# Local attention in windows of 64: tokens moved in groups of 512, stores moved to the loads' queue

## The chip, the cores and the metric

One Trainium2 chip, one of its cores. The metric is device time in microseconds (us), lower is better. Engines: PE (matmul), DVE (VectorE), ACT (ScalarE), POOL (GpSimd), SP (SyncE), and 16 DMA engines. The runs were made in several calls, on different chips: the median of the kernel before moved between 973.7 and 974.3 us, so differences under 1 us between calls are not read.

## The reference

```python
B, S, D, W = 4, 4096, 1536, 64           # q, k, v: float32 [B, S, D]
logits = einsum('bnwd,bnud->bnwu', q_w, k_w) * D ** -0.5   # inside each window of 64 tokens
attn = softmax(logits)
out = einsum('bnwu,bnud->bnwd', attn, v_w)                 # float32 [B, S, D]
```

There is little arithmetic per byte: 302 MB are read and 101 MB written, 402.7 MB together.

## The kernel before

A step handles a pair of windows, 128 tokens. GpSimd issues the three loads, which cast float32 to bf16 on the way. PE transposes q and k in chunks, DVE and ACT evict the transposes from PSUM, PE makes logits, ACT the exponentials, PE the product with v, DVE and ACT scale it, and SP issues the store.

```python
qkv_pool = tile_pool(name="qkv", bufs=3)
for b in range(B):
    for p in range(n_pairs):
        s0 = p * PAIR
        ...
        nc.gpsimd.dma_start(out=q_nat, in_=q[b, s0 : s0 + PAIR, :])   # [128, D] bf16 <- f32
        nc.gpsimd.dma_start(out=k_nat, in_=k[b, s0 : s0 + PAIR, :])
        nc.gpsimd.dma_start(out=v_nat, in_=v[b, s0 : s0 + PAIR, :])
        ...                                     # 24 transposes into tp, eight to a PSUM tile
            if g % 2 == 0: nc.vector.tensor_copy(qk_t[:, lo:hi, :], tp[:, : hi - lo, :])
            else:          nc.scalar.copy(qk_t[:, lo:hi, :], tp[:, : hi - lo, :])
        ...                                     # logits, exp, sum, product with v, scaling
        nc.sync.dma_start(out=out[b, s0 : s0 + PAIR, :], in_=o_sb)
```

The softmax here doesn't subtract the row's maximum and nothing guards it: scores larger than these inputs give would overflow.

Of the kernel before, what the change touches and what calls it, by code (L numbers as in the profile page):

```python
# [1 line left out]

# [5 lines left out]


FP32 = mybir.dt.float32
BF16 = mybir.dt.bfloat16


@with_exitstack
def kernel(
    ctx: ExitStack,
    tc: tile.TileContext,
    q: bass.AP,
    k: bass.AP,  # L20
    v: bass.AP,
    out: bass.AP,
):
    nc = tc.nc

    B, S, D = q.shape
    W = 64
    PAIR = 2 * W
    n_pairs = S // PAIR
    n_chunks = D // 128  # L30
    n_out_chunks = D // 512
    scale = float(D) ** -0.5

    consts = ctx.enter_context(tc.tile_pool(name="consts", bufs=1))
    qkv_pool = ctx.enter_context(tc.tile_pool(name="qkv", bufs=3))
    qkt_pool = ctx.enter_context(tc.tile_pool(name="qkt", bufs=2))
    attn_pool = ctx.enter_context(tc.tile_pool(name="attn", bufs=4))
    out_pool = ctx.enter_context(tc.tile_pool(name="outp", bufs=3))

    tp_psum = ctx.enter_context(tc.tile_pool(name="tp_psum", bufs=3, space=bass.MemoryType.PSUM))  # L40
    s_psum = ctx.enter_context(tc.tile_pool(name="s_psum", bufs=2, space=bass.MemoryType.PSUM))
    u_psum = ctx.enter_context(tc.tile_pool(name="u_psum", bufs=3, space=bass.MemoryType.PSUM))

    ident = consts.tile([128, 128], BF16)
    make_identity(nc, ident)

    maskt = consts.tile([128, 128], BF16)
    nc.gpsimd.memset(maskt, -100000.0)
    nc.gpsimd.memset(maskt[0:64, 0:64], 0.0)
    nc.gpsimd.memset(maskt[64:128, 64:128], 0.0)  # L50

    ones = consts.tile([128, 1], BF16)
    nc.gpsimd.memset(ones, 1.0)

    for b in range(B):
        for p in range(n_pairs):
            s0 = p * PAIR

            q_nat = qkv_pool.tile([128, D], BF16, name="q_nat")
            k_nat = qkv_pool.tile([128, D], BF16, name="k_nat")  # L60
            v_nat = qkv_pool.tile([128, D], BF16, name="v_nat")
            nc.gpsimd.dma_start(out=q_nat, in_=q[b, s0 : s0 + PAIR, :])  # L62
            nc.gpsimd.dma_start(out=k_nat, in_=k[b, s0 : s0 + PAIR, :])  # L63
            nc.gpsimd.dma_start(out=v_nat, in_=v[b, s0 : s0 + PAIR, :])  # L64

            qk_t = qkt_pool.tile([128, 2 * n_chunks, 128], BF16, name="qk_t")
            n_groups = (2 * n_chunks + 7) // 8
            for g in range(n_groups):
                lo = g * 8
                hi = min(lo + 8, 2 * n_chunks)  # L70
                tp = tp_psum.tile([128, 8, 128], BF16, name="tp")
                for c in range(lo, hi):
                    if c < n_chunks:
                        src = q_nat[:, c * 128 : (c + 1) * 128]
                    else:
                        cc = c - n_chunks
                        src = k_nat[:, cc * 128 : (cc + 1) * 128]
                    nc.tensor.transpose(tp[:, c - lo, :], src, ident)  # L78
                if g % 2 == 0:
                    nc.vector.tensor_copy(qk_t[:, lo:hi, :], tp[:, : hi - lo, :])  # L80
                else:
                    nc.scalar.copy(qk_t[:, lo:hi, :], tp[:, : hi - lo, :])  # L82

            s_ps = s_psum.tile([128, 132], FP32, name="s_ps")
            st = s_ps[:, 0:128]
            for j in range(n_chunks):
                nc.tensor.matmul(  # L87
                    st,
                    qk_t[:, n_chunks + j, :],
                    qk_t[:, j, :],  # L90
                    start=(j == 0),
                    stop=False,
                )
            nc.tensor.matmul(st, ident, maskt, start=False, stop=True)  # L94

            p_t = attn_pool.tile([128, 128], BF16, name="p_t")
            nc.scalar.activation(  # L97
                out=p_t,
                in_=st,
                func=mybir.ActivationFunctionType.Exp,  # L100
                scale=scale,
            )

            nc.tensor.matmul(s_ps[:, 128:129], p_t, ones, start=True, stop=True)  # L104
            r_recip = attn_pool.tile([128, 1], FP32, name="r_recip")
            nc.vector.reciprocal(r_recip, s_ps[:, 128:129])  # L106

            o_sb = out_pool.tile([128, D], FP32, name="o_sb")
            for c in range(n_out_chunks):
                u_ps = u_psum.tile([128, 512], FP32, name="u_ps")  # L110
                nc.tensor.matmul(  # L111
                    u_ps,
                    p_t,
                    v_nat[:, c * 512 : (c + 1) * 512],
                    start=True,
                    stop=True,
                )
                o_slice = o_sb[:, c * 512 : (c + 1) * 512]
                if c % 2 == 0:
                    nc.scalar.mul(o_slice, u_ps, r_recip)  # L120
                else:
                    nc.vector.tensor_scalar_mul(o_slice, u_ps, r_recip)  # L122

            nc.sync.dma_start(out=out[b, s0 : s0 + PAIR, :], in_=o_sb)


# [1 line left out]
_INS = ['q', 'k', 'v']  # L128
_OUTS = [((4, 4096, 1536), 'float32')]


# [23 lines left out]
```

## Time and profile before

| | before |
|---|---|
| median time | 974.3 us |
| span in the profile | 972.3 us |
| HBM rate over the span | 414 GB/s |
| DMA engines busy | 9 tenths or more in all slices but the last |
| PE, ACT, DVE busy | 59%, 33%, 30% |

These are lines of the page of the kernel before. The DMA row has one digit per fortieth of the span, in tenths busy. The queue lines give packets, MB on the SBUF side of casting loads, and the time that the packets list as a share of 16 engines' span.

```profile
span 972.3 us, 12982 instructions
...
DMA  9999999999999999999999999999999999999997
...
DMA packets 73788, 252.52 MB, mean 260 GB/s; under 512 B 8192, under 2 KB 8192, under 8 KB 73728
...
q0 software_dynamic: 55296, 151.02, 79.2%
q1 hardware_dynamic: 18432, 100.67, 26.2%
...
HBM read 301.99 MB, written 100.66 MB: 414 GB/s over the span
...
L80 DVE COPY qk_t<-tp 128x1024 bf16<-128x1024 bf16 x256 | 176.9, 691 | 455.6 <-PE tp L78 452.2
...
L82 ACT COPY qk_t<-tp 128x1024 bf16<-128x1024 bf16 x128 | 129.4, 1011 | 90.3 <-PE s_ps L104 82.9
```

The DMA row is full and no other engine is. q0 is GpSimd's queue (loads), q1 is SP's (stores). Each has one small completion packet for every eight data packets: 49152 + 6144 and 16384 + 2048, the 8192 packets under 512 bytes.

Waits of the same kernel: who waited for whom, total us, times, longest.

```profile
POOL v_nat L64 <- PE u_ps L111: 464.1, 71, 8.3
...
PE tp L78 <- DMA q_nat<-in_q_dram: 326.9, 128, 6.4
```

PE waits for loads. GpSimd waits for PE to free a buffer, but by then two pairs are queued, so its wait starves nothing.

Windows of the same kernel: stretch and length in us, then busy time of each engine, the granted clock, the DMA share and GB/s.

```profile
200.00:500.00 300.00, 178.59 (x1634) 138.24 (x1631) 90.33 (x160) 99.08 (x160) 63.58 (x120) 0.73 1.07 263
955.00:972.00 17.00, 9.03 (x80) 6.20 (x78) 4.74 (x9) 6.45 (x11) 0.00 (x0) 0.80 0.70 215
```

The steady stretch has a DMA share of 1.07, over 1 because the packets of an engine overlap in the records: a load packet lists 248 ns, and the next starts some 230 ns after it. The last 17 us reach 0.70: there the last pairs are computed and stored with little left to move.

### The profile page before, as it was taken

What the parts mean: (1) busy time and instruction counts of PE and PEld (TensorE: products, weight loads), DVE (VectorE), ACT (ScalarE), POOL (GpSimd) and SP (SyncE); (2) the same over time, 40 slices, a digit from 0 to 9 for tenths busy, and PEclk for the clock granted to TensorE, in tenths of its full rate; (3) what the DMA queues carried; (4) which work ended last, traced back from release to release, by engine and by line L of the source; (5) the groups of instructions that cost most, each with busy time, mean ns of one, the idle gap of its engine ahead of it and who ended that gap; (6) DMA issues with size and microseconds to landing.
All of it is one profiled execution on the core that took longest, in us unless ns stands there. A gap on an engine that the chain in (4) does not pass through costs nothing. (4 is left out here: it accounts for less than half of the span.)

```text
span 972.3 us, 12982 instructions
## 1 busy us (share of the span) xinstructions
PE 571.3 (59%) x5248; PEld 442.4 (46%) x5248; DVE 289.5 (30%) x512; ACT 317.7 (33%) x513; POOL 204.7 (21%) x394
## 2 busy tenths in 40 slices
PE   4666655655657556565565654647556556566564
PEld 3454443444445445444454443445445445444443
DVE  2223322323223232332332322323233232332332
ACT  2333333333333333333333333334333333333333
POOL 4111212112221121112211211112211122121210
PEclk9676777768676786777777778786776776776777
DMA  9999999999999999999999999999999999999997
GB/s 180 266 259 268 258 267 263 255 274 253 265 266 258 269 259 259 261 265 266 259 261 273 256 262 263 256 275 259 258 270 257 266 259 257 271 260 261 262 261 233
DMA packets 73788, 252.52 MB, mean 260 GB/s; under 512 B 8192, under 2 KB 8192, under 8 KB 73728
## 3 DMA queue, kind: packets, MB, share of 16 engines
q0 software_dynamic: 55296, 151.02, 79.2%
q1 hardware_dynamic: 18432, 100.67, 26.2%
q8 instruction: 41, 0.67, 0.2%
q14 instruction: 19, 0.16, 0.0%
HBM read 301.99 MB, written 100.66 MB: 414 GB/s over the span
## 5 line engine op out<-in xcount | busy, mean ns | idle before, releaser
L78 PE MATMUL tp<-ident,q_nat 128*128 128x128 bf16 x1536 | 180.4, 275 | 326.9 <-DMA q_nat<-in_q_dram 326.9
L80 DVE COPY qk_t<-tp 128x1024 bf16<-128x1024 bf16 x256 | 176.9, 691 | 455.6 <-PE tp L78 452.2
L78 PEld LDWEIGHTS <-q_nat 128*128 128x128 bf16 x1536 | 132.2, 126 | 353.0 <-DMA q_nat<-in_q_dram 352.5
L64 POOL DMA_DIRECT2D v_nat<-in_v_dram x128 | 68.1, 532 | 669.1 <-PE u_ps L111 464.1
L78 PE MATMUL tp<-ident,k_nat 128*128 128x128 bf16 x1536 | 162.5, 256 | 66.3 <-DMA k_nat<-in_k_dram 65.8
L97 ACT ACTIVATE p_t<-s_ps 128x128 bf16<-128x128 f32 x128 | 35.5, 278 | 497.4 <-PE s_ps L94 497.4
L78 PEld LDWEIGHTS <-k_nat 128*128 128x128 bf16 x1536 | 127.5, 117 | 137.6 <-DMA k_nat<-in_k_dram 88.8
L120 ACT ACTIVATE o_sb<-u_ps,r_recip 128x512 f32<-128x512 f32 x256 | 164.8, 689 | 62.0 <-DVE r_recip L106 38.0
L87 PE MATMUL s_ps<-qk_t 128*128 128x128 bf16 x1536 | 175.6, 283 | 2.1 <-ACT qk_t L82 1.3
L82 ACT COPY qk_t<-tp 128x1024 bf16<-128x1024 bf16 x128 | 129.4, 1011 | 90.3 <-PE s_ps L104 82.9
L87 PEld LDWEIGHTS <-qk_t 128*128 128x128 bf16 x1536 | 146.1, 134 | 5.7 <-ACT qk_t L82 5.7
L111 PE MATMUL u_ps<-v_nat,p_t 128*128 128x512 bf16 x384 | 142.6, 495 | 0.0
L122 DVE TENSOR_SCALAR o_sb<-u_ps,r_recip 128x512 f32<-128x512 f32 x128 | 96.1, 750 | 52.5 <-PE u_ps L111 52.5
L63 POOL DMA_DIRECT2D k_nat<-in_k_dram x128 | 68.8, 538 | 69.7 <-DMA v_nat<-in_v_dram 60.9
L106 DVE RECIPROCAL r_recip<-s_ps 128x1 f32<-128x1 f32 x128 | 21.4, 167 | 170.2 <-PE s_ps L104 170.2
L62 POOL DMA_DIRECT2D q_nat<-in_q_dram x128 | 68.9, 538 | 4.7 <-issue 2.7
L111 PEld LDWEIGHTS <-p_t 128*128 128x128 bf16 x384 | 35.3, 116 | 25.6 <-issue 18.3
L94 PE MATMUL s_ps<-maskt,ident 128*128 128x128 bf16 x128 | 36.0, 282 | 0.0
L104 PE MATMUL s_ps<-ones,p_t 128*128 128x1 bf16 x128 | 24.4, 190 | 0.6 <-ACT p_t L97 0.4
L94 PEld LDWEIGHTS <-ident 128*128 128x128 bf16 x128 | 17.2, 134 | 0.0
L104 PEld LDWEIGHTS <-p_t 128*128 128x128 bf16 x128 | 15.3, 119 | 2.3 <-ACT p_t L97 2.1
L82 ACT ACT_TABLE_LOAD x1 | 1.3, 1283 | 0.7 <-PEq L139 0.7
(10 smaller groups left out, 1.5 us busy)
## 6 DMA issues: line engine op xcount, KB each, us to landing
out_dram<-o_sb SPq DMA_DIRECT2D x128, 768.0 KB, 7.8
q_nat<-in_q_dram POOLq DMA_DIRECT2D x128, 384.0 KB, 17.7
k_nat<-in_k_dram POOLq DMA_DIRECT2D x128, 384.0 KB, 19.2
v_nat<-in_v_dram POOLq DMA_DIRECT2D x128, 384.0 KB, 16.1
```

What stands on the lines that cost most here:

```text
L62: nc.gpsimd.dma_start(out=q_nat, in_=q[b, s0 : s0 + PAIR, :])
L63: nc.gpsimd.dma_start(out=k_nat, in_=k[b, s0 : s0 + PAIR, :])
L64: nc.gpsimd.dma_start(out=v_nat, in_=v[b, s0 : s0 + PAIR, :])
L78: nc.tensor.transpose(tp[:, c - lo, :], src, ident)
L80: nc.vector.tensor_copy(qk_t[:, lo:hi, :], tp[:, : hi - lo, :])
L82: nc.scalar.copy(qk_t[:, lo:hi, :], tp[:, : hi - lo, :])
L87: nc.tensor.matmul(st, qk_t[:, n_chunks + j, :], qk_t[:, j, :], start=(j == 0), stop=False,)
L94: nc.tensor.matmul(st, ident, maskt, start=False, stop=True)
L104: nc.tensor.matmul(s_ps[:, 128:129], p_t, ones, start=True, stop=True)
L111: nc.tensor.matmul(u_ps, p_t, v_nat[:, c * 512 : (c + 1) * 512], start=True, stop=True,)
L120: nc.scalar.mul(o_slice, u_ps, r_recip)
L122: nc.vector.tensor_scalar_mul(o_slice, u_ps, r_recip)
```

## The change

The intent is to feed the DMA engines better: fewer and larger DMAs, longer packets for q and k, and one queue for nearly all traffic. Four pairs, 512 tokens, form a group. q and k are loaded so that partition p holds the four consecutive tokens 4p to 4p+3, 24576 contiguous bytes of HBM. The copy that evicts a transpose then puts columns back in token order, with a stride of four elements. v and the output keep token order in rows of 6144 bytes. The last group of all is moved pair by pair.

```diff
-    qkv_pool = ... bufs=3
+    qkv_pool = ... bufs=2
+        src = lambda t: t[b, s0 : s0 + toks, :].rearrange("(g p) d -> p g d", p=128)
+        rows = lambda t: t[b, s0 : s0 + toks, :].rearrange("(p g) d -> p g d", p=128)
+        if not LAST:
+            nc.gpsimd.dma_start(out=q_nat, in_=rows(q))
+            nc.gpsimd.dma_start(out=k_nat, in_=rows(k))
+            nc.gpsimd.dma_start(out=v_nat, in_=src(v))
...                                              # LAST: one DMA per pair and tensor, as before
+        qk_by_row = qk_t4.rearrange("d c (p g) -> d c p g", g=GROUP)
-                    nc.vector.tensor_copy(qk_t[:, lo:hi, :], tp[:, : hi - lo, :])
+                    to = qk_by_row[:, lo:hi, :, g]          # LAST: contiguous
+                    nc.vector.tensor_copy(to, tp[:, : hi - lo, :])
...
-            nc.sync.dma_start(out=out[b, s0 : s0 + PAIR, :], in_=o_sb)
+    # GpSimd issues in this order: loads 0, 1, then loads n + 2 before store n
+    with tc.manual_schedule(engines={mybir.EngineType.Pool}):
+        loaded = {n: load(n) for n in range(2)}
+        for n in range(total):
+            o_sb = compute(n, *loaded.pop(n))    # LAST: stores its pairs from SP
+            if n + 2 < total:
+                loaded[n + 2] = load(n + 2)
+            if n < total - 1:
+                nc.gpsimd.dma_start(out=dst, in_=o_sb)
```

## The prediction

> **What bounds the kernel now.** The DMA engines. The slice rows of the page show DMA at 9 tenths or more in 39 of 40 slices; the windows view gives a DMA share of 1.06 to 1.07 from 20 to 955 us. PE is busy 59%, ACT 33%, DVE 30%; in the waits view PE waits 327 us for q and 66 us for k, and GpSimd waits for buffers. HBM traffic is 302 MB read and 101 MB written, 402.7 MB.
>
> In the trace's packet records every data packet carries one row of 6144 HBM bytes (49152 loads, 16384 stores, 4096 per engine) and lists 248 ns; the engine's next packet starts about 230 ns after the last. Over 30 to 955 us the stream costs 234.6 ns per engine and data packet: 233.4 with loads alone, 236.5 where half are stores. I put the 3 to 4 ns over 230 down to the 8192 completion packets of 4 bytes (22 ns each). The Trainium skill, "DMA: Bandwidth & Descriptors", section "Where 436 GB/s comes from", states a ceiling of 435 GB/s: 925 us for these bytes, 226 ns a packet. The trace's steady 419 GB/s agrees that little is left. Besides there are 3.2 us before the first packet and a tail: after 955 us the share is 0.70, some 5 us lost.
>
> **What the change does.** 512 tokens per DMA, not 128: 384 load and 128 store issues become about 105 and 35. q and k go with 24576 contiguous bytes per partition, so four packets become one, if they aren't cut up again; v and stores keep 6144-byte rows. Stores move from the SP queue to the GpSimd queue. Bytes, matmuls and copies stay equal in number. The copies that evict transposes now write with a stride of 8 bytes: the DVE one (691 ns now) probably loses its fast rate, to an estimated 1.1 us; 256 x 0.4 = 100 us more DVE work, off the critical path.
>
> Is compute still hidden? Four pairs need some 30 us of DMA (128 packets per engine x 230 ns). PE needs 571/32 = 18 us; with waits between phases I estimate 20 to 24. GpSimd asks for q and k of group n+2 when the transposes of n are done, so a group of DMA work is always queued. I expect no idle DMA.
>
> **The sum.** Completion packets fall to about a quarter: -2.5 ns per packet. Long q and k packets: -1.5 ns. One queue in place of two may save 1 ns. So 229.3 to 231 ns x 4096 = 939 to 946 us, plus 3.2 us of start and about 2 us of tail, since the last group goes pair by pair while two large stores drain. The gain is on the critical path, which is DMA throughput.
>
> Predicted 948 us (-2.7%), range 937 to 963. Faster by over 2%: 0.70; within 2%: 0.24; slower: 0.06.
>
> **What would show it.** DMA at 9 in all slices; far fewer packets, q0 carrying the stores; steady HBM rate 424 to 429 GB/s; DVE copies near 1.1 us; PE still waiting mostly for DMA; last slices full. If q and k packets stay at 6144 bytes, 1.5 ns of the gain goes (954 us at most).
>
> **What would make it wrong.** Stores in the software queue could serialise with loads worse than two queues do; [...]strided copies slower than 1.5 us would stretch a group past 29 us; the queue may hold too little, leaving DMA idle at group boundaries.

## The result, and the profile after

The changed kernel takes 956.4 us (median of 8 runs, 955.7 to 957.1), against 974.3. The ratio is 0.982, interval 0.981 to 0.983: 1.8% faster. Ratios here are the mean time of one kernel's runs over that of the other's in the same rounds, so not quite the ratio of the medians quoted.

Lines of the page of the changed kernel:

```profile
span 953.9 us, 12350 instructions
...
DMA  8999999999999999999999999999999999999997
...
DMA packets 44023, 252.45 MB, mean 265 GB/s; under 512 B 2240, under 2 KB 2240, under 8 KB 36032
...
q0 software_dynamic: 43392, 248.52, 101.4%
q1 hardware_dynamic: 576, 3.15, 0.8%
...
HBM read 301.99 MB, written 100.66 MB: 422 GB/s over the span
...
DMA 44%; DVE 23%; issue 15%; PE 9%; ACT 4%; POOL 2%; ACTq 0%; POOLq 0%; DVEq 0%
...
L110 DVE COPY qk_t<-tp 128x1024 bf16<-128x1024 bf16 x256 | 577.1, 2399 | 67.0 <-PE tp L104 66.8
L112 ACT COPY qk_t<-tp 128x1024 bf16<-128x1024 bf16 x128 | 305.4, 2386 | 236.7 <-PE tp L104 236.7
```

DMA is still full. Packets fell from 73788 to 44023: completions from 8192 to 2240, and most of the 32768 packets of q and k became a quarter as many. SP's queue is almost empty. The strided copies take 2.4 us where 0.7 (DVE) and 1.0 (ACT) were needed; DVE is now busy 72% of the span. The line after the HBM rate is the page's chain of work that ended last, as shares of the span: it runs through DVE for 23%. Whether the copies therefore cost time is a question for an experiment (the second below).

Waits, then windows, of the changed kernel:

```profile
POOL q_nat L74 <- PE tp L104: 387.7, 29, 27.2
...
PE tp L104 <- DMA k_nat<-in_k_dram: 82.8, 27, 5.8
...
PE tp L104 <- DVE qk_t L110: 77.0, 98, 1.7
```

```profile
200.00:500.00 300.00, 193.74 (x1673) 155.38 (x1674) 220.51 (x162) 158.88 (x164) 25.95 (x40) 0.64 1.03 267
940.00:951.00 11.00, 0.00 (x0) 0.00 (x0) 0.00 (x0) 0.00 (x0) 0.00 (x0) 0.50 0.60 253
```

PE waits for loads far less than before and a good deal for copies, yet in 27 of the groups it still meets the DMA of k: the group's compute ends some 3 us before its next data. After 940 us no engine computes; only stores drain, and not all DMA engines take part.

**Where the time went.** The trace records every DMA packet. From these I computed, for each run, the HBM bytes moved between 30 and 920 us, and from that the *steady cost*: the time that one engine needs for 6144 bytes. Each engine moves 4096 times as much, so steady cost x 4096 is the stream. What is left of the span I call the ends: the start, the draining, and the time after the last packet.

| | steady cost | stream | ends | span |
|---|---|---|---|---|
| before | 234.8 ns | 961.6 us | 10.7 us | 972.3 us |
| changed | 230.1 ns | 942.4 us | 11.5 us | 953.9 us |

The stream gave 19.2 us and the ends took 0.8 back. The measured time lies about 2 us above the span for both kernels. Each steady cost comes from one profile. The changed kernel and three kernels with the same stream (its repetition and the two runs on the ends, below) give 230.0 to 230.2 ns, so the steady cost repeats within some 0.2 ns; the ends do not repeat so well (11.5 and 11.9 us for the changed kernel).

### The profile page after: what moved, and what is told of

Read it like the earlier page. It is cut to its first block, busy times and chain, and to the rows that moved or that the text cites. A ratio compares the mean times of both kernels' runs of the same rounds, so it can differ in the third digit from the quotient of the medians. Undisturbed runs are those within 1.5% of the kernel's fastest.

```text
span 953.9 us, 12350 instructions
## 1 busy us (share of the span) xinstructions
PE 588.2 (62%) x5248; PEld 468.1 (49%) x5248; DVE 688.7 (72%) x512; ACT 497.4 (52%) x513; POOL 88.1 (9%) x146
## 2 busy tenths in 40 slices
DMA packets 44023, 252.45 MB, mean 265 GB/s; under 512 B 2240, under 2 KB 2240, under 8 KB 36032
## 4 chain that ended last, share of the span: by engine, by line
DMA 44%; DVE 23%; issue 15%; PE 9%; ACT 4%; POOL 2%; ACTq 0%; POOLq 0%; DVEq 0%
DMA k_nat<-in_k_dram 44%; DVE qk_t L110 22%; PE s_ps L125 4%; PE u_ps L148 3%; ACT o_sb L157 3%; PE tp L104 1%; DVE o_sb L159 1%; POOL out_dram L177 1%; ACT p_t L135 1%; POOL q_nat L74 1%; POOL v_nat L76 0%; PE s_ps L142 0%; PE s_ps L132 0%; ACT qk_t L112 0%; DVE r_recip L144 0%
## 5 line engine op out<-in xcount | busy, mean ns | idle before, releaser
L110 DVE COPY qk_t<-tp 128x1024 bf16<-128x1024 bf16 x256 | 577.1, 2399 | 67.0 <-PE tp L104 66.8
L112 ACT COPY qk_t<-tp 128x1024 bf16<-128x1024 bf16 x128 | 305.4, 2386 | 236.7 <-PE tp L104 236.7
L104 PE MATMUL tp<-ident,k_nat 128*128 128x128 bf16 x1536 | 181.5, 289 | 123.4 <-DMA k_nat<-in_k_dram 82.8
L104 PE MATMUL tp<-ident,q_nat 128*128 128x128 bf16 x1536 | 160.8, 273 | 117.8 <-ACT qk_t L112 67.8
L104 PEld LDWEIGHTS <-k_nat 128*128 128x128 bf16 x1536 | 148.8, 134 | 138.9 <-DMA k_nat<-in_k_dram 87.5
L148 PE MATMUL u_ps<-v_nat,p_t 128*128 128x512 bf16 x384 | 132.6, 449 | 3.5 <-ACT o_sb L157 2.4
L76 POOL DMA_DIRECT2D v_nat<-in_v_dram x31 | 23.3, 752 | 332.8 <-PE u_ps L148 310.3
L74 POOL DMA_DIRECT2D q_nat<-in_q_dram x31 | 17.0, 548 | 387.7 <-PE tp L104 387.7
L148 PEld LDWEIGHTS <-p_t 128*128 128x128 bf16 x384 | 33.7, 109 | 18.1 <-issue 11.6
L177 POOL DMA_DIRECT2D out_dram<-o_sb x31 | 23.5, 758 | 16.3 <-ACT o_sb L157 7.5
L75 POOL DMA_DIRECT2D k_nat<-in_k_dram x31 | 16.9, 544 | 46.3 <-PE tp L104 43.8
```

The source lines that it names most:

```text
L74: nc.gpsimd.dma_start(out=q_nat, in_=rows(q))
L104: nc.tensor.transpose(tp[:, c - lo, :], src_c, ident)
L110: nc.vector.tensor_copy(to, tp[:, : hi - lo, :])
L112: nc.scalar.copy(to, tp[:, : hi - lo, :])
L148: nc.tensor.matmul(u_ps, p_t, v_nat[:, g, c * 512 : (c + 1) * 512], start=True, stop=True,)
L177: nc.gpsimd.dma_start(out=dst, in_=o_sb)
```

## The experiments

Three things changed at once in the stream: grouping (fewer completions), packet length of q and k, and the number of queues. Grouping also means longer runs of loads and of stores, and one queue also means that stores come in order behind loads and not beside them; the runs do not part these. The theory gave each a share (completions 2.5 ns, length 1.5, queue up to 1). The rival, P in the expectations, came from a fit of the packet records after the result: the second queue is worth most, long packets come next, completions almost nothing.

### q and k in short packets, order and strided copies kept

```diff
-        q_nat = qkv_pool.tile([128, GROUP, D], BF16, name="q_nat")      # k_nat alike
+        q_nat = qkv_pool.tile([128, GROUP, D + 16], BF16, name="q_nat")
-            nc.gpsimd.dma_start(out=q_nat, in_=rows(q))
+            nc.gpsimd.dma_start(out=q_nat[:, :, :D], in_=rows(q))
```

> q and k in the order of the change (row p holds tokens 4p to 4p+3, strided copies kept), but each SBUF row padded by 32 bytes, so that a partition's 24576 bytes go as four packets of 6144. Theory P (packet cost, from a fit of the two traces: a long packet 907 ns, four short ones 922): 512 x 15 ns = 8 us slower than the changed kernel, 964 us. Theory C (as the prediction split it: 6 us for long packets, the rest completions and queue): 962 us. Theory G (only fewer, larger issues count): 956 us.

Measured: 958.5 us, 2.1 more than the changed kernel, and correct. Steady cost 231.1 ns: 1.0 ns more, 4 us of stream, of which 1.3 came back at the ends (10.2 us). Both theories had the length too dear, P the more: 1.0 x 4096 / 512 is 8 ns for a long packet, not 15.

### q and k in token order: short packets and plain copies

```diff
-            nc.gpsimd.dma_start(out=q_nat, in_=rows(q))                  # k alike
+            nc.gpsimd.dma_start(out=q_nat, in_=src(q))
-                    to = qk_by_row[:, lo:hi, :, g]
+                    to = qk_t4[:, lo:hi, g * 128 : (g + 1) * 128]
```

> q and k in token order like v, so short packets and no strided copies (DVE and ACT copies back to 0.7 and 1.0 us from 2.4). If the strided copies are wholly off the critical path, the same time as the kernel with padded rows, within 1 us. If they cost something in spite of the DMA bound, this one is faster by more than 2 us.

Measured: 959.3 us, steady cost 231.3 ns. The lines with the plain copies (groups view):

```profile
L110 DVE COPY qk_t<-tp 128x1024 bf16<-128x1024 bf16 x256 | 173.0, 690 | 529.4 <-PE tp L104 528.7
...
L112 ACT COPY qk_t<-tp 128x1024 bf16<-128x1024 bf16 x128 | 129.5, 1012 | 552.4 <-PE tp L104 552.4
```

The run to compare with is the one before, which has the same packets and strided copies: 958.5 us. With 404 us less DVE work and 176 us less ACT work than in the changed kernel, this one is 0.8 us slower, not faster. The strided copies are off the critical path in spite of being more than twice as slow as predicted, and the 23% of DVE in the chain above was no time to be won.

### The large stores from SP again

```diff
-                nc.gpsimd.dma_start(out=dst, in_=o_sb)
+                nc.sync.dma_start(out=dst, in_=o_sb)
```

> The changed kernel with its large stores issued from SP, not GpSimd: two queues again. Theory P (the fit gives a store packet 239 ns in the second queue and 231 in the shared one): 1024 x 8 ns = 8 us slower than the changed kernel, 964 us. Theory C (at most 1 ns per packet for the one queue): 956 to 960. Theory G: 956. Perhaps 2 us come back at the end, as the span then ends sooner after the last packet.

Measured: 963.9 us, 7.5 more than the changed kernel, as P expected. Steady cost 232.9 ns, 2.8 ns more; the ends are shorter (8.1 us), which gives back 3.4 of the 11.6 us of stream. The prediction's 1 ns for the queue falls. Page lines of this run, queues and HBM rate:

```profile
q0 software_dynamic: 27024, 151.00, 76.1%
q1 hardware_dynamic: 16944, 100.67, 26.3%
...
HBM read 301.99 MB, written 100.66 MB: 419 GB/s over the span
```

Bytes and packets are those of the changed kernel; only the queue differs, and the rate falls from 422 to 419 GB/s.

### v and the output in long packets too (wrong result)

```diff
-            nc.gpsimd.dma_start(out=v_nat, in_=src(v))
+            nc.gpsimd.dma_start(out=v_nat, in_=rows(v))
-                dst = out[...].rearrange("(g p) d -> p g d", p=128)
+                dst = out[...].rearrange("(p g) d -> p g d", p=128)
```

> Wrong result on purpose: v and the stores also go with 24576 contiguous bytes per partition. Theory P: 2 x 512 long packets in place of 4 short ones, 15 ns saved each, 940 us. Theory C (3 ns per short packet saved on the other half): 950. Theory G: 956.

Measured: 947.7 us. Its output is wrong, which doesn't matter for the time. Steady cost 228.6 ns, 1.5 less than the changed kernel (6.2 us). The expectation of P had an error of arithmetic: v and the output make 512 long packets per engine together, not 2 x 512, so P should have said 949. This run therefore does not part the theories. It does show that some 9 us more were to be had if v and the output could be laid out so.

### Grouping alone, and the single queue alone

From the kernel with short packets and plain copies, once with the stores from SP, once with pairs in place of groups:

```diff
 grouping alone:      -  nc.gpsimd.dma_start(out=dst, in_=o_sb)
                      +  nc.sync.dma_start(out=dst, in_=o_sb)
 single queue alone:  -GROUP = 4             +GROUP = 1
                      -  bufs=2, load(n + 2)  +  bufs=3, load(n + 3)
```

> Groups of four as in the change, but short q and k packets in token order and the large stores from SP: of the change only the grouping is left. If the parts add up (2 to 3 us for short packets, 7.5 us for the second queue, both measured), 966 us. My prediction's term for completion packets alone (2.5 ns x 4096 = 10 us) says 964; if grouping does nothing by itself, 974.

> One pair per load and store as in the kernel before, short packets, but loads and stores all from GpSimd in the order of the change: of the change only the single queue is left. Theory Q (the second queue costs a store packet some 8 ns): 974 - 8 to 11 = 963 to 966 us, steady cost per engine and packet about 232 ns against 234.8. If the single queue only helps with large DMAs: 974, or slower where GpSimd waits in order.

Measured: grouping alone 971.9 us, only 2.5 gained; the parts do not add up to 966. The single queue alone 967.1 us, 7.2 gained, in its predicted direction and nearly its size. Now all six combinations exist. Each cell is the median time and the steady cost:

| | two queues | one queue |
|---|---|---|
| pairs, short packets | 974.3 us, 234.8 ns (before) | 967.1 us, 232.6 ns |
| groups, short packets | 971.9 us, 234.0 ns | 959.3 us, 231.3 ns |
| groups, long q and k | 963.9 us, 232.9 ns | 956.4 us, 230.1 ns (changed) |

The queue is worth 2.2 to 2.8 ns in every row, long packets 1.1 to 1.2 in both columns, grouping 0.8 with two queues and 1.3 with one. In steady cost the parts add up within 0.7 ns. In time they do not, because the ends vary: they are 10.7, 11.4 and 8.1 us in the left column, 11.8, 10.3 and 11.5 in the right.

To see why grouping gives so little, I sorted the microseconds from 30 to 920 (without those in which instructions were fetched) by the share of stores among the packets in progress:

| steady cost, ns | loads alone | 40 to 60% stores |
|---|---|---|
| before | 232.3 | 236.0 |
| groups, short, two queues | 230.4 | 236.1 |
| pairs, short, one queue | 232.0 | 231.9 |
| groups, short, one queue | 230.1 | 231.1 |
| changed | 228.7 | 230.3 |

The cells move by some 0.2 ns with the way of counting. With loads alone, grouping saves 1.9 ns; that is (1/8 - 1/32) of a completion packet, so 20 ns for one, close to the 22 that it lists. But wherever both queues have work, a packet costs 236 ns whether completions are many or few. With two queues the saving is lost in half of the time.

### Copies alone: is it the queue, the direction, or the alternation?

Both kernels give a wrong result. The first stores 25 MB from SP, then 25 MB from GpSimd, then loads beside stores in two queues, then in one. The second loads in two queues at once, stores in two queues at once, loads from SP alone (no cast there) and stores from GpSimd alone. A memset of the moved tile parts the stages.

```diff
+            nc.sync.dma_start(out=dst(0, n), in_=o_sb)                    # stage 1, 8 times
+            nc.gpsimd.dma_start(out=dst(1, n), in_=o_sb)                  # stage 2
+            loads(2, n); nc.sync.dma_start(out=dst(2, n), in_=o_sb)       # stage 3
+            loads(3, n); nc.gpsimd.dma_start(out=dst(3, n), in_=o_sb)     # stage 4
```

> Wrong result on purpose; DMA copies alone in four stages parted by a memset of the stored tile: 25 MB of stores from SP, 25 MB of stores from GpSimd, then 75 MB of loads beside 25 MB of stores in two queues, then the same in one queue. If the second queue's descriptors are slow by themselves, stores alone from SP cost about 239 ns per packet and engine and from GpSimd 231. If it is the alternation between two queues, both stages alone cost the same (230 to 232) and only the mixed stage with two queues costs more, 235 or over while both queues have work, against 231 in the last stage.

```diff
+            nc.gpsimd.dma_start(out=q_nat, in_=rows(q, 0, n)); nc.sync.dma_start(out=o[n % 2], in_=rows(k, 0, n))
+            nc.sync.dma_start(out=rows(out, 0, n), in_=o[0]); nc.gpsimd.dma_start(out=rows(out, 1, n), in_=o[1])
+            nc.sync.dma_start(out=o[n % 2], in_=rows(v, 0, n))
+            nc.gpsimd.dma_start(out=rows(out, b, n), in_=o[n % 2])        # b = 2, 3
```

> Wrong result on purpose; copies alone in stages parted by memsets: loads in two queues at once (GpSimd and SP), stores in two queues at once, loads from SP alone, stores from GpSimd alone. If alternating between two queues costs by itself (6 ns a packet), loads in two queues cost 236 ns per packet and engine against 230 alone. If it is load and store side by side from two queues, loads in two queues cost 230, like loads alone. Stores from GpSimd alone, 50 MB of them: 236 to 239 as in the earlier copies, if sustained stores alone are slower than stores between loads (231).

Windows of the first kernel. The columns after the length are busy time of GpSimd, granted clock, DMA share and GB/s, where a casting load counts with its 3072 bytes. The stretches are SP stores alone, GpSimd stores alone, both queues, loads alone, and one queue with both:

```profile
16.00:60.00 44.00, 0.00 (x0) 1.00 1.01 415
112.00:136.00 24.00, 0.00 (x0) 1.00 1.02 418
160.00:250.00 90.00, 4.45 (x6) 1.00 1.05 313
272.00:400.00 128.00, 19.62 (x21) 1.00 1.08 214
430.00:600.00 170.00, 13.40 (x19) 1.00 1.06 268
```

Windows of the second: loads in two queues, stores in two queues, loads from SP alone, stores from GpSimd alone:

```profile
12.00:114.00 102.00, 4.45 (x6) 1.00 1.05 313
150.00:240.00 90.00, 0.00 (x0) 1.00 1.01 414
282.00:312.00 30.00, 0.00 (x0) 1.00 1.01 417
342.00:414.00 72.00, 5.21 (x7) 1.00 1.01 411
```

In ns per packet and engine, from the packet records:

| stage | cost |
|---|---|
| casting loads alone, GpSimd | 230.0 |
| casting loads and stores in one queue | 231.0 |
| casting loads and stores in two queues, half and half | 235.8 |
| casting loads (GpSimd) and plain loads (SP), half and half | 235.8 |
| plain loads alone, SP | 235.3 |
| stores alone, SP | 235.6 to 237.6 |
| stores alone, GpSimd | 235.6 to 239.7 |
| stores in two queues, half and half | 235.5 to 238.3 |

One answer is clear. SP's packets are not dearer than GpSimd's: stores alone cost as much from either. The expectation of 230 to 232 for stores alone missed, and this leaves the rest open. A transfer with 6144 bytes on both sides costs 235 to 240 when it runs alone for long, in one queue too. Half of those and half casting loads would make 233 to 235 if the costs simply averaged. Where the two kinds meet in two queues, loads beside loads come 3 ns over that, loads beside stores 1 to 3, so a mix of directions is not needed. But stores in two queues cost no more than stores in one, so no cost of two queues by themselves shows there. That it takes two queues and two kinds of packet fits these runs, but is not shown: no run has plain and casting loads in one queue. Nor do they tell why stores between loads in one queue come at 231, and so cheaper than stores alone.

### The ends

The second attempt to win time went to the ends: first loads ahead of the constants, and the last two large stores from SP.

```diff
+        loaded = {n: load(n) for n in range(2)}
+        ident = consts.tile(...) ...             # moved down, below the first loads
-                nc.gpsimd.dma_start(out=dst, in_=o_sb)
+                eng = nc.gpsimd if n < total - 3 else nc.sync
+                eng.dma_start(out=dst, in_=o_sb)
```

> The changed kernel with its first loads issued before the constants are made (first packet 1.3 us earlier) and the last two large stores issued from SP (3.3 us lie between the last packet and the end of the span with GpSimd, 1.2 to 2 with SP). If these ends are what my sum missed: 956.4 - 1.3 - 1 to 2 = 953 to 954 us. If the start hides behind the stream or the tail is set by the slower half of the engines alone: 955 to 956.

Measured: 956.9 us, a miss. Windows of the end:

```profile
900.00:940.00 40.00, 23.47 (x209) 17.45 (x210) 17.25 (x22) 15.89 (x24) 3.17 (x6) 0.67 1.04 309
940.00:956.00 16.00, 6.35 (x44) 4.42 (x45) 3.13 (x6) 3.93 (x6) 0.00 (x0) 0.61 0.45 152
```

PE still works 6.35 us after 940, where it had nothing left to do in the changed kernel. The reading, argued from these windows only, is that SP's stores shared the DMA engines with the last loads in place of queueing behind them, so the last pairs came late, and their compute and store stood alone at the end. Draining cost 4 us more than in the changed kernel, more than the start (0.6) and the time after the last packet (2.0) gave.

So the next one keeps the early loads and sends every store, those of the last group too, from GpSimd, behind all loads. It ran beside the unaltered changed kernel.

```diff
-                nc.sync.dma_start(out=out[b, s0 + g * PAIR : ...], in_=o_sb[:, g, :])
+                nc.gpsimd.dma_start(out=out[b, s0 + g * PAIR : ...], in_=o_sb[:, g, :])
```

> The changed kernel with its first loads ahead of the constants, and all stores, those of the last group too, from GpSimd behind everything else. The earlier attempt at the ends showed the start worth 0.6 us and the two-queue end 4 us worse; this keeps the first and not the second: 955 to 955.5 us, 1 us under the changed kernel run in the same call. If the start is hidden: the same time.

> The changed kernel unaltered, as a yardstick on the same chip: 956.4 us, within 0.7.

Measured: 953.8 us (953.5 to 954.1, 4 runs), and 955.7 us (955.5 to 957.4, 5 runs) for the changed kernel. It beats both kernels; its ratio to the kernel before is 0.979 (0.978 to 0.981). First issues on GpSimd in the timeline of the changed kernel, then of this one:

```profile
1.76 0.11 POOL L56 MEMSET ones<- 128x1 bf16 x1
1.80 0.68 POOL L74 DMA_DIRECT2D q_nat<-in_q_dram  x1
```

```profile
0.74 1.28 ACT L101 ACT_TABLE_LOAD   x1 [0.74 <-PEq L192]
1.27 0.67 POOL L63 DMA_DIRECT2D q_nat<-in_q_dram  x1 [0.83 <-POOLq L192]
```

The first load goes out 0.5 us earlier. The rest of the gain lies after the last packet: 1.4 us to the end of the span, where the changed kernel has 3.3 in both its profiles. What the core waits for in these 1.9 us I did not find out, and this edit need not be what removed them: q and k in short packets and q and k in token order, whose ends are written as in the changed kernel, have 1.5 us there.

## Why the prediction was right or wrong

The time fell within the range (937 to 963), 8 us above the point of 948. The gain is 1.8%, just short of the 2% to which 0.70 was given. By point:

- **DMA throughput is the bound, before and after.** Right: the DMA row stays at 9, and taking the strided copies away gains nothing.
- **Compute stays hidden.** Right, by a smaller margin than estimated. A strided copy takes 2.4 us, not 1.1. A group needs some 26 us of compute in the trace (479 to 505 us), against 29.3 from one arrival of k to the next. The prediction's own alarm, that copies over 1.5 us would stretch a group past 29 us, was set wrong. So was "PE still waiting mostly for DMA": in the waits view PE waits 96 us for loads and some 226 us for the copies that empty the transposes (DVE 153, ACT 73).
- **Steady cost 229.3 to 231 ns.** Right in sum: 230.1, and partly by luck, since the terms were mis-sized in opposite directions. Completions: 2.5 ns forecast, 0.8 to 1.3 measured for grouping. The prediction put all of the 3 to 4 ns over 230 down to them; that nearly holds with loads alone (232.3 before, 1.9 saved by grouping), not where both queues work, since there a packet costs 236 with few completions too. Long packets: 1.5 forecast, 1.0 to 1.2 measured. One queue: up to 1 forecast, 2.2 to 2.8 measured. The largest term was the one least believed in.
- **3.2 us of start and 2 us of tail.** This is the step that failed, and nearly all of the distance to the point. The ends of the span measure 11.5 us, not 5: the stream starts as if at 4.0 us, draining loses 4.2, and 3.3 pass after the last packet. Another 2 us lie outside the span. Together that is the 8 us. The tail did not improve as forecast, since the DMA engines do not finish together: in the packet records only 8 of 16 are busy from 946 to 948 us.

The same arithmetic applied to the kernel before would have shown the gap at once: 234.6 x 4096 = 961 us, plus 3.2, plus 5, is 969, not 974. Had I subtracted the forecast saving from the measured 974.3 us, 3.6 to 5.3 ns x 4096, I would have said 953 to 960.

The Trainium skill, "DMA: Bandwidth & Descriptors", section "Why small descriptors are slow (HBM only)", states a fixed overhead of about 3 cycles per packet, and the section that the prediction cites has 32 bytes a cycle at 850 MHz. An estimate from these, taking a packet of the trace for a packet of the page, is 195 cycles, 229.4 ns, for 6144 bytes and 771 cycles, 907.1 ns, for 24576. So long packets save an estimated 10.6 ns per four rows. The trace agrees for casting loads: 230.0 for short ones alone, and 909 in the microseconds of the changed kernel in which only long packets move, a saving of 11; the steady costs of the pairs of runs, stores and all, give 8 to 9. It does not agree for plain packets alone, which cost 235 to 240.

## What to carry to other kernels

When the DMA engines are full, count what a byte costs them: packets, completions, and whether a second queue works at the same time. Here one queue for casting loads and stores was worth more in steady cost (2.2 to 2.8 ns) than longer packets or fewer DMAs, though why is open, and stores alone lost nothing in two queues. Forecast from the measured time minus the difference, not from a sum of parts that was never checked against the kernel before. Look at the end separately: two stores moved beside the last loads cost 4 us of draining here. It is no rule, since with all large stores in SP's queue the ends were the shortest of all (8.1 us).

## What the Trainium skill lacked or had wrong

- "DMA: Bandwidth & Descriptors", section "Issuing engines are not separate DMA queues", says that DMAs issued from different engines run on the same 16 engines and that issuing from several only saves sequencer time. It lacks that two queues at work can cost throughput: 235.8 ns per packet and engine against 231.0 in one queue where casting loads meet stores in the copies, and 7 us of 974 in the kernel when only the queue changes. For stores alone it showed no such cost (235.5 to 238.3 in two queues, 235.6 to 239.7 in one).
- No page that I read has the cost of plain transfers beside casting ones: 235 to 240 ns for 6144 bytes on both sides, running alone, against 230.0 for loads that cast to half the bytes.
- "DMA: Bandwidth & Descriptors" also advises batching DMAs to 1 MiB for 75% of the peak or more. It has no figure for what batching is worth when several DMAs are queued all the time. Here loads of 0.4 MB and stores of 0.8 MB already ran at 414 GB/s, and going to 1.5 and 3 MB gained 2.5 us of 974 with two queues and 7.8 us of 967 with one.
- "SBUF — State Buffer", section "Door 1: The DMA port swizzle", says that an engine's access needs at least two hits per 16-byte line for full bandwidth. A bf16 write with a stride of 8 bytes has two, and still a 128x1024 copy from PSUM took 2.4 us on DVE and on ACT, where contiguous ones took 0.69 and 1.01 us. What it is in the stride that costs this, no run here parts.
- The same DMA page says that engines 7 and 15 are usually slower. The packet records here do not number the engines, so this is not tested; but at the end of the changed kernel, in both its profiles, the late ones are half of the 16 and not two: some 8 finish at 943 to 946 us and the others at 948 to 951.
